# Sums of u and low parts of h in the second feed-forward: reordered between ScalarE and VectorE, first inner sums two products later

## The chip, the cores and the metric

The kernel runs on one NeuronCore of a Trainium2 chip. The metric is the device time of one execution in microseconds; the median of several runs stands for a kernel. TensorE (PE in the profile) multiplies matrices into PSUM banks, VectorE (DVE) and ScalarE (ACT) do the elementwise work, GpSimd (POOL) and SyncE (SP) mostly issue transfers. Each engine works through its own instructions in order and waits on semaphores for the others.

## The reference

One decoder block over 512 tokens of width 1024, all in float32: a SwiGLU feed-forward, a token mixer (pooling and dilated attention), and a second SwiGLU feed-forward, each on a modulated RMSNorm of the residual h, and a final RMSNorm. What the change touches is the feed-forward (inner width 2816):

```python
def swiglu(u, w_in, w_out):
    a, b = jnp.split(u @ w_in, 2, axis=-1)
    return (jax.nn.silu(a) * b) @ w_out

def reference(...):
    ...
    u = modulate(rmsnorm(h, g_norm_ffn2[l]), sh3, sc3)
    h = h + 0.5 * gt3 * swiglu(u, w_ffn2_in[l], w_ffn2_out[l])
    return rmsnorm(h, g_final)
```

## The kernel before

**Float32 products from high and low parts.** Every operand of TensorE is kept as a rounded part ("high", written by ScalarE as a copy to a narrower type) and the rest ("low", which VectorE gets by subtracting the high part). A product is three matmuls: high by high, high by low, low by high. So each weight tile costs one ScalarE copy (`whi`, line 312) and one VectorE subtraction (`wlo`, line 326), and so does each activation: u as `UH`/`UL`, the inner activation h as `HI`/`HK`. For weights of the second feed-forward that are not needed soon, ScalarE and a GpSimd transfer make the low part instead (line 308 and 310). All data is laid with features on the 128 partitions and the 512 tokens along the columns.

**A Strassen-like scheme with seven products.** Most inner tiles are not computed plainly. Two tiles at once (a "duo") are seen as a 2 by 2 block product, blocks of weights by blocks of u (two halves of the features by two halves of the tokens, 256 each). Instead of eight block products it needs seven, at the price of sums: four sums of weight blocks (line 251, VectorE, `X<-...`), four sums of blocks of u (line 699, once, since all duos share them), and the recombination of the results. The sums of u need high and low parts too: `SH`/`SL`, lines 705 and 706, and for the fourth one, which goes back into a part of `UH`/`UL`, lines 708 and 709. The second feed-forward does its output product in the same way ("quad", `out_quad`), from sums of four inner tiles ("inner sums", `h_sums`, lines 828 to 834), whose parts are `ut`, `G` and a half of `HI`/`HK`.

**The start of the second feed-forward** (`ffn2`). `head` computes four banks, the two halves a and b of inner tiles 0 and 1, plainly. Inner tiles 2 and 3 follow plainly (`ffn_tile`, 24 matmuls of 512 columns for each half), while VectorE forms the sums of u for the duos. For each of the tiles 0 to 3, `ffn_post` multiplies silu(a) by b on VectorE (`mult`, line 664), makes the high part on ScalarE (line 666) and the low part on VectorE (line 667). The list of steps that `u_steps` returns (first `whole`: u put together again from its parts for two blocks, line 715; then the four sums with their parts) is worked off between them: two steps after tile 0, three after tile 1, the rest while TensorE is in tile 2. The last step, the parts of the fourth sum, is called `last` and runs in the first duo after its product 0.

**The first duo** (inner tiles 4 and 5). Its seven products are numbered 0 to 6. They go to three PSUM banks A, B, C: A, B, A, C, A, B, A. After product 0 ScalarE copies A to C, after product 1 it copies B to SBUF (`p5`), after products 2 and 4 it copies A to SBUF (`u2`, `u3`: rows `u<-bank`), after 3 and 6 it takes the silu of C and A. The bank A goes on being accumulated, so product 2 can't begin before the copy of A to C is done, product 4 not before that of `u2`, product 6 not before that of `u3`.

**What sets the order.** The order is written by hand: each engine gets its instructions in the order in which the Python code issues them. `look` runs the weight splits three or four weight tiles ahead. `later(n, f)` puts work after the n-th product from now, and `step`, called after each product and ahead of that product's copies, runs what is due. `h_sums` puts its first sum at 2, and then one sum with the neighbouring high and low parts at each of 3 to 6. It is called once before the duo that comes ahead of each output quad: for quad 0 that is the first duo.

```python
        for n, what in enumerate(((lambda: add(h22, h21, h22, OP.add),),
                                  (lambda: high(0, h22), lambda: add(h21, h11, h21, OP.subtract), lambda: low(0, h22)),
                                  ...
            for f in what:
                self.later(2 + n, f)
```

Loads of weights are issued by SyncE into a few raw buffers. Two of them are the places of the blocks a12 and a22 of u; they can be used for weights once `last` is done.

The first feed-forward also calls `u_steps`; there one step is worked off after each of its first eight output tiles.

Of the kernel before, what the change touches and what calls it, by code (L numbers as in the profile page):

```python
# [11 lines left out]
AF = mybir.ActivationFunctionType  # L12
OP = mybir.AluOpType
# [130 lines left out]
class Kernel:  # L144
# [513 lines left out]

    def ffn_post(self, j, s, pb):
        nc = self.nc
        h = self.kept[j // 2 % 3][:, j % 2 * T:j % 2 * T + T] if self.kept else self.fw.tile([P, T], F32, name=("hf", "u3")[j % 2])
        nc.vector.tensor_tensor(h, s, pb, op=OP.mult)
        hh, hl = self.HH[j % NH], self.HL[j % NH]
        nc.scalar.activation(hh, h, AF.Copy)
        nc.vector.tensor_tensor(hl, h, hh, op=OP.subtract)

    def ffn_silu(self, j, pa):
        s = self.fw.tile([P, T], F32, name="sl" if j % 2 == 0 else "u2" if not self.kept else "p5")  # L670
# [22 lines left out]
    def u_steps(self, n):  # L693

        nc, v = self.nc, self.nc.vector
        (a11, a12), (a21, a22) = self.U4

        def add(o, x, y, op):
            return lambda: v.tensor_tensor(o, x, y, op=op)

        def split(i, u):
            def f():
                hi, lo = self.S[i]
                if i < 3:
                    nc.scalar.activation(hi, u, AF.Copy)
                    v.tensor_tensor(lo, u, hi, op=OP.subtract)
                    return
                nc.scalar.activation(hi, u.rearrange("p (k t) -> p k t", k=4), AF.Copy)
                v.tensor_tensor(lo, u.rearrange("p (k t) -> p k t", k=4), hi, op=OP.subtract)
            return f  # L710

        def whole(u, k):
            x = slice(k, k + 4)
            hi, lo = (y.rearrange("p (k t) -> p k t", k=KT)[:, x, :HT] for y in (self.UHv, self.ULv))
            return lambda: v.tensor_tensor(u.rearrange("p (k t) -> p k t", k=4), hi, lo, op=OP.add)

        last = split(3, a12)
        return ([whole(a11, 0), whole(a12, 4)] if n else []) + [add(a22, a21, a22, OP.add), split(0, a22), add(a21, a11, a21, OP.subtract), split(2, a21),
                add(a11, a22, a11, OP.subtract), split(1, a11), add(a12, a12, a11, OP.subtract)], last

    def step(self):

# [94 lines left out]
    def h_sums(self, k0):  # L817

        nc, v = self.nc, self.nc.vector
        half = lambda x, h: x.rearrange("p (j h t) -> p j h t", j=2, h=2)[:, :, h, :]  # L820
        a, b = (self.kept[k // 2 % 3] for k in (k0, k0 + 2))
        h11, h21, h12, h22 = half(a, 0), half(a, 1), half(b, 0), half(b, 1)
        x = slice(k0 % NH * T, (k0 % NH + 2) * T)
        r = lambda x: x.rearrange("p (j t) -> p j t", j=2)
        to = [(r(h), r(l)) for h, l in self.G] + [(half(self.HHall[:, x], 1), half(self.HLall[:, x], 1))]

        def add(o, x, y, op):
            v.tensor_tensor(o, x, y, op=op)

        def high(i, s):  # L830
            nc.scalar.activation(to[i][0], s, AF.Copy)

        def low(i, s):
            v.tensor_tensor(to[i][1], s, to[i][0], op=OP.subtract)

        for n, what in enumerate(((lambda: add(h22, h21, h22, OP.add),),
                                  (lambda: high(0, h22), lambda: add(h21, h11, h21, OP.subtract), lambda: low(0, h22)),
                                  (lambda: high(2, h21), lambda: add(h11, h22, h11, OP.subtract), lambda: low(2, h21)),
                                  (lambda: high(1, h11), lambda: add(h12, h12, h11, OP.subtract), lambda: low(1, h11)),
                                  (lambda: high(3, h12), lambda: low(3, h12)))):  # L840
            for f in what:
                self.later(2 + n, f)

    def out_quad(self, k0, gate):

# [56 lines left out]
    def ffn2(self):  # L902
        self.put, self.now = [], 0
        self.kept = [self.cond, self.cs, self.AR]
        bk = [self.nb() for _ in range(4)]
        self.head(2, bk, AF.Silu)
        self.G = [(self.tp.tile([P, T], F32R, name="ut"), self.fw.tile([P, T], F32R, name=f"G{i}")) for i in range(3)]
        self.todo, last = self.u_steps(2)
        do = lambda n: [self.todo.pop(0)() for _ in range(n)]
        for j in range(2):  # L910
            self.ffn_post(j, self.ffn_silu(j, bk[2 * j]), bk[2 * j + 1])
            do(2 + j)
        pa = self.ffn_tile()
        do(len(self.todo))
        self.ffn_post(2, self.ffn_silu(2, pa), self.ffn_tile())
        self.ffn_pair(3)
        self.ffn(2, 4, last)

    def open_ffn(self):
# [766 lines left out]
```

## Time and profile before

| | |
|---|---|
| median of 3 runs | 1012.51 us (1011.1 to 1012.77) |
| the profiled execution, its own time | 1010.66 us |
| its span in the profile | 1008.8 us |
| VectorE busy in the span | 788.6 us (78%) |
| ScalarE busy | 496.4 us (49%) |
| GpSimd busy | 47.3 us (5%) |
| chain of waits that ended last | TensorE 90%, VectorE 7%, ScalarE 1% |

TensorE is busy for nearly the whole span. Engine names in rows are PE, DVE, ACT, POOL and SP (SPq: SyncE's issues of transfers). In a timeline row stand the start in us, the duration, the engine, the line of the kernel, the operation, the tile that is written, the tiles that are read, and in brackets how long the engine was idle before and who ended that. A row of the list of waits has the total, the number of times and the longest. A row of a stretch has the length, the busy time of TensorE, its weight loads, VectorE, ScalarE and GpSimd with the number of instructions, then the granted clock of TensorE (1.00 is full), the busy share of the transfers, and GB/s.

### The profile page before, as it was taken

How to read it: one execution, taken by the hardware profiler on the slowest of the kernel's cores; microseconds unless marked ns; L12 is line 12 of the kernel's file. 1: busy time of each engine (PE TensorE's matmuls, PEld its weight loads, DVE VectorE, ACT ScalarE, POOL GpSimd, SP SyncE). 2: the span in 40 equal slices, each digit the busy share in tenths (PEclk: the TensorE clock that was granted, in tenths of full speed). 3: DMA queues.
4: the chain of work that ended last, by engine and by line, in shares of the span. 5: the costliest groups of instructions: out<-in, count | busy, mean ns of one | idle time of the engine just before them, and what ended most of it. 6: DMA issues, size and time to landing. Idle time of an engine off the chain costs nothing.

```text
span 1008.8 us, 16370 instructions
## 1 busy us (share of the span) xinstructions
PE 994.6 (99%) x6652; PEld 913.9 (91%) x6652; DVE 788.6 (78%) x1182; ACT 496.4 (49%) x754; POOL 47.3 (5%) x54
## 2 busy tenths in 40 slices
PE   8999999999999999999999999999899999999997
PEld 6888898989999999889988888898899999999996
DVE  7978879889787676879447777567998988989754
ACT  6443253625434552233414333463677768677652
POOL 0000000000000000007100000000011011011001
PEclk9999999999999999999999999999999999999998
DMA  9866456555533413122054774322467666756712
GB/s 341 275 224 228 140 195 189 175 164 185 168 99 117 145 46 99 58 84 84 32 185 161 272 261 134 92 78 63 146 147 178 177 147 155 201 130 164 178 32 84
DMA packets 46574, 152.24 MB, mean 151 GB/s; under 512 B 5281, under 2 KB 8609, under 8 KB 46498
## 3 DMA queue, kind: packets, MB, share of 16 engines
q1 hardware_dynamic: 42354, 137.95, 41.3%
q0 software_dynamic: 3456, 12.58, 7.5%
q8 instruction: 52, 0.85, 0.3%
q10 hardware_dynamic: 688, 0.66, 0.2%
q14 instruction: 24, 0.20, 0.1%
HBM read 148.40 MB, written 2.77 MB: 150 GB/s over the span
## 4 chain that ended last, share of the span: by engine, by line
PE 90%; DVE 7%; ACT 1%; issue 1%; DMA 0%; DVEq 0%; ACTq 0%
PE bank L357 14%; PE bank L358 14%; PE bank L359 14%; PE bank L739 10%; PE bank L741 9%; PE bank L740 9%; PE bank L867 3%; PE bank L866 3%; PE bank L865 3%; DVE wlo L326 1%; PE bank L1616 1%; PE bank L1620 1%; PE bank L1618 1%; PE bank L1212 1%; PE bank L1391 1%; PE bank L1392 1%
## 5 line engine op out<-in xcount | busy, mean ns | idle before, releaser
L326 DVE TENSOR_TENSOR wlo<-raw,whi 128x1024 fp32r<-128x1024 f32 (+7 forms) x157 | 156.7, 1011 | 56.0 <-ACT whi L312 55.8
L312 ACT ACTIVATE whi<-raw 128x1024 fp32r<-128x1024 f32 (+7 forms) x172 | 150.6, 894 | 31.2 <-DVE raw L251 27.6
L357 PE MATMUL bank<-UH,whi 128*128 128x512 f32 (+1 forms) x432 | 158.0, 366 | 0.0
L358 PE MATMUL bank<-UL,whi 128*128 128x512 f32 (+1 forms) x432 | 154.0, 357 | 0.1
L359 PE MATMUL bank<-UH,wlo 128*128 128x512 f32 (+1 forms) x432 | 153.9, 356 | 0.0
L741 PE MATMUL bank<-UH,wlo 128*128 128x256 f32 x512 | 141.6, 277 | 0.0
L739 PE MATMUL bank<-UH,whi 128*128 128x256 f32 x512 | 141.5, 276 | 0.0
L740 PE MATMUL bank<-UL,whi 128*128 128x256 f32 x512 | 141.5, 276 | 0.0
L326 DVE TENSOR_TENSOR wlo<-X,whi 128x1024 fp32r<-128x1024 f32 (+4 forms) x102 | 111.4, 1099 | 30.8 <-ACT whi L312 30.5
L312 ACT ACTIVATE whi<-X 128x1024 fp32r<-128x1024 f32 (+4 forms) x111 | 105.6, 966 | 40.6 <-DVE X L251 39.6
L739 PE MATMUL bank<-SH,whi 128*128 128x256 f32 x384 | 108.0, 281 | 3.0 <-ACT u L746 2.2
L740 PE MATMUL bank<-SL,whi 128*128 128x256 f32 x384 | 107.6, 280 | 0.0
L741 PE MATMUL bank<-SH,wlo 128*128 128x256 f32 x384 | 107.5, 280 | 0.0
L357 PE MATMUL bank<-HI,whi 128*128 128x512 f32 (+1 forms) x278 | 96.8, 348 | 0.0
L358 PE MATMUL bank<-HK,whi 128*128 128x512 f32 (+1 forms) x278 | 96.5, 347 | 0.0
L740 PEld LDWEIGHTS bank<-UL,whi 128*128 128x128 f32 x512 | 96.2, 188 | 0.2
L359 PE MATMUL bank<-HI,wlo 128*128 128x512 f32 (+1 forms) x278 | 96.4, 347 | 0.0
L741 PEld LDWEIGHTS bank<-UH,wlo 128*128 128x128 f32 x512 | 96.1, 188 | 0.2 <-DMA wlo<-wf2i 0.2
L739 PEld LDWEIGHTS bank<-UH,whi 128*128 128x128 f32 x512 | 96.1, 188 | 0.2
L359 PEld LDWEIGHTS bank<-UH,wlo 128*128 128x128 f32 x432 | 81.1, 188 | 12.1
L358 PEld LDWEIGHTS bank<-UL,whi 128*128 128x128 f32 x432 | 81.2, 188 | 11.7 <-issue 0.5
L357 PEld LDWEIGHTS bank<-UH,whi 128*128 128x128 f32 x432 | 81.2, 188 | 11.2 <-issue 0.5
(300 smaller groups left out, 2104.1 us busy)
## 6 DMA issues: line engine op xcount, KB each, us to landing
ada<-wada SPq DMA_DIRECT2D x47, 512.0 KB, 5.3
raw<-wmix SPq DMA_DIRECT2D x44, 512.0 KB, 4.1
raw<-wf1i SPq DMA_DIRECT2D x34, 512.0 KB, 4.5
raw<-wf2i SPq DMA_DIRECT2D x30, 512.0 KB, 3.7
wlo<-wf2i POOLq DMA_DIRECT2D x16, 512.0 KB, 6.3
X<-wf2i SPq DMA_DIRECT2D x14, 512.0 KB, 4.3
cs<-wada SPq DMA_DIRECT2D x12, 512.0 KB, 3.7
AR<-wada SPq DMA_DIRECT2D x12, 512.0 KB, 4.4
```

The source lines that it names most:

```text
L312: self.nc.scalar.activation(self.hi[:, y], r[:, x], AF.Copy)
L326: self.nc.vector.tensor_tensor(self.lo[:, y], r[:, x], self.hi[:, y], op=OP.subtract)
L357: M(ps, hi, uh, start=start, stop=False)
L358: M(ps, hi, ul, start=False, stop=False)
L359: M(ps, lo, uh, start=False, stop=stop)
L739: M(o, hi, uh, start=start and p == 0 and k == 0, stop=False, skip_group_check=True)
L740: M(o, hi, ul, start=False, stop=False, skip_group_check=True)
L741: M(o, lo, uh, start=False, stop=k == 3, skip_group_check=True)
L865: M(o, hi, uh, start=start and m % 2 == 0 and k == 0, stop=False, skip_group_check=True)
L866: M(o, hi, ul, start=False, stop=False, skip_group_check=True)
L867: M(o, lo, uh, start=False, stop=k == 1, skip_group_check=True)
L1212: M(o, pt[:, blk * P:blk * P + P], v, start=i == 0, stop=i == len(srcs) - 1)
```

## The change

The computation is the same. Three things move.

`ffn_post` takes a function `between`, which gets the low part of h as a thing to be done and decides when. For tiles 0 and 1 one step of the sums of u comes ahead of the low part; for tile 2 it comes after the first half of tile 3 has been issued, for tile 3 after product 0 of the first duo.

`u_steps` no longer issues the high and the low part of a sum one after the other: the high part is followed by the next sum, and the low part comes one step later. The number of steps stays, and so the first feed-forward gets the new order too.

`h_sums` starts after product 4 from its call instead of 2, for quad 0 alone.

```diff
-    def ffn_post(self, j, s, pb):
+    def ffn_post(self, j, s, pb, between=None):
...
         nc.scalar.activation(hh, h, AF.Copy)
-        nc.vector.tensor_tensor(hl, h, hh, op=OP.subtract)
+        low = lambda: nc.vector.tensor_tensor(hl, h, hh, op=OP.subtract)
+        if between is None:
+            return low()
+        between(low)
...
+        def high(i, u):
+            return lambda: nc.scalar.activation(self.S[i][0], four(i, u), AF.Copy)
+
+        def low(i, u):
+            return lambda: v.tensor_tensor(self.S[i][1], four(i, u), self.S[i][0], op=OP.subtract)
+
+        def both(*fs):
+            return lambda: [f() for f in fs]
...
-        return ([whole(a11, 0), whole(a12, 4)] if n else []) + [add(a22, a21, a22, OP.add), split(0, a22), add(a21, a11, a21, OP.subtract), split(2, a21),
-                add(a11, a22, a11, OP.subtract), split(1, a11), add(a12, a12, a11, OP.subtract)], last
+        return ([whole(a11, 0), whole(a12, 4)] if n else []) + [
+            add(a22, a21, a22, OP.add), both(high(0, a22), add(a21, a11, a21, OP.subtract)),
+            both(high(2, a21), low(0, a22)), add(a11, a22, a11, OP.subtract), both(high(1, a11), low(2, a21)),
+            add(a12, a12, a11, OP.subtract), low(1, a11)], both(high(3, a12), low(3, a12))
...
-                self.later(2 + n, f)
+                self.later((2 if k0 else 4) + n, f)
...
         for j in range(2):
-            self.ffn_post(j, self.ffn_silu(j, bk[2 * j]), bk[2 * j + 1])
-            do(2 + j)
+            self.ffn_post(j, self.ffn_silu(j, bk[2 * j]), bk[2 * j + 1], lambda low: (do(1), low(), do(1 + j)))
         pa = self.ffn_tile()
         do(len(self.todo))
-        self.ffn_post(2, self.ffn_silu(2, pa), self.ffn_tile())
-        self.ffn_pair(3)
+        due = []
+        self.ffn_post(2, self.ffn_silu(2, pa), self.ffn_tile(), due.append)
+        pa = self.ffn_tile()
+        due.pop()()
+        self.ffn_post(3, self.ffn_silu(3, pa), self.ffn_tile(), lambda low: self.later(1, low))
         self.ffn(2, 4, last)
```

How the instructions now stand shows at three places. The lines of the changed file are a few higher (699 is 702, 706 is 710, 746 is 750, 831 is 835).

VectorE at the start of the second feed-forward, from the first `whole` on, before (`cond` holds h of tiles 0 and 1, `X` the blocks of u, `HK`, `SL` and `wlo` are low parts):

```order
L715 TENSOR_TENSOR X<-UH,UL 128x1024 x2
L664 TENSOR_TENSOR cond<-p_5891,bank_100 128x512
L667 TENSOR_TENSOR HK<-cond,HI 128x512
L699 TENSOR_TENSOR X<-X 128x1024
L706 TENSOR_TENSOR SL_5609<-X,SH_5608 128x1024
L699 TENSOR_TENSOR X<-X 128x1024
L326 TENSOR_TENSOR wlo<-raw_67,whi 128x1024
L706 TENSOR_TENSOR SL_5614<-X,SH_5613 128x1024
```

And the same piece with the change:

```order
L718 TENSOR_TENSOR X<-UH,UL 128x1024
L667 TENSOR_TENSOR HK<-cond,HI 128x512
L718 TENSOR_TENSOR X<-UH,UL 128x1024
L664 TENSOR_TENSOR cond<-p_5891,bank_100 128x512
L702 TENSOR_TENSOR X<-X 128x1024
L667 TENSOR_TENSOR HK<-cond,HI 128x512
L702 TENSOR_TENSOR X<-X 128x1024
L710 TENSOR_TENSOR SL_5609<-X,SH_5608 128x1024
L326 TENSOR_TENSOR wlo<-raw_67,whi 128x1024
L702 TENSOR_TENSOR X<-X 128x1024
L710 TENSOR_TENSOR SL_5614<-X,SH_5613 128x1024
```

Between each multiplication or sum and its low part now stands one other operation.

ScalarE in the first duo, from the copy after product 1 (`p_6025`) to the silu after product 3 (`sl`), before; `ut` is the high part of an inner sum, `whi` that of a weight:

```order
L746 ACTIVATE p_6025<-bank_100 128x512
L312 ACTIVATE whi<-X 128x1024
L831 ACTIVATE ut<-cs 128x512
L746 ACTIVATE u_6026<-bank_99 128x2x256
L312 ACTIVATE whi<-X 128x1024
L831 ACTIVATE ut<-cond 128x512
L769 ACTIVATE sl<-bank_101 128x2x256
```

With the change, up to the copy after product 4 (the second `u_6025`):

```order
L750 ACTIVATE p_6024<-bank_100 128x512
L312 ACTIVATE whi<-X 128x1024
L750 ACTIVATE u_6025<-bank_99 128x2x256
L312 ACTIVATE whi<-X 128x1024
L773 ACTIVATE sl<-bank_101 128x2x256
L312 ACTIVATE whi<-X 128x1024
L835 ACTIVATE ut<-cs 128x512
L750 ACTIVATE u_6025<-bank_99 128x2x256
```

The high part of the first inner sum stood ahead of the copy after product 2 and now stands ahead of the copy after product 4.

ScalarE at the seam of the duo and the output quad, from the silu after product 6 to the quad's first copies from bank to bank (line 848), before:

```order
L769 ACTIVATE sl<-bank_99 128x2x256
L312 ACTIVATE whi<-X 128x896
L312 ACTIVATE whi<-X 128x128
L848 ACTIVATE bank_101<-bank_102 128x512
L848 ACTIVATE bank_100<-bank_97 128x512
```

With the change:

```order
L773 ACTIVATE sl<-bank_99 128x2x256
L312 ACTIVATE whi<-X 128x896
L312 ACTIVATE whi<-X 128x128
L835 ACTIVATE HI<-cs 128x2x256
L852 ACTIVATE bank_101<-bank_102 128x512
L852 ACTIVATE bank_100<-bank_97 128x512
```

The high part of the last inner sum has come in ahead of the two copies. TensorE, GpSimd and SyncE have the same instructions in the same order as before.

More of the change, by code (lines that the diff above doesn't have):

```diff
@@ L699, in add @@
             return lambda: v.tensor_tensor(o, x, y, op=op)
[L701 to L710, printed above, removed]
+        four = lambda i, u: u.rearrange("p (k t) -> p k t", k=4) if i == 3 else u
+        def high(i, u):
[4 more added lines that the diff above has]
+            return lambda: [f() for f in fs]
         def whole(u, k):
@@ L715, in whole @@
             return lambda: v.tensor_tensor(u.rearrange("p (k t) -> p k t", k=4), hi, lo, op=OP.add)
-        last = split(3, a12)
-        return ([whole(a11, 0), whole(a12, 4)] if n else []) + [add(a22, a21, a22, OP.add), split(0, a22), add(a21, a11, a21, OP.subtract), split(2, a21),
-                add(a11, a22, a11, OP.subtract), split(1, a11), add(a12, a12, a11, OP.subtract)], last
+        return ([whole(a11, 0), whole(a12, 4)] if n else []) + [
+            add(a22, a21, a22, OP.add), both(high(0, a22), add(a21, a11, a21, OP.subtract)),
+            both(high(2, a21), low(0, a22)), add(a11, a22, a11, OP.subtract), both(high(1, a11), low(2, a21)),
+            add(a12, a12, a11, OP.subtract), low(1, a11)], both(high(3, a12), low(3, a12))
     def step(self):
```

## The prediction

> **What bounds the kernel now.** I read the page first, then who waited for whom on TensorE, then the timeline of TensorE around the two waits found there.
>
> ```profile
> span 1008.8 us, 16370 instructions
> PE bank L1538 <- ACT cond L1536: 3.3, 1, 3.3
> PE bank L739 <- ACT u L746: 2.2, 1, 2.2
> PE bank L739 <- ACT bank L746: 0.8, 1, 0.8
> PE bank L1189 <- ACT prob L1177: 0.3, 1, 0.3
> PE bank L443 <- ACT ut L510: 0.3, 1, 0.3
> PE bank L1616 <- ACT UH L472: 0.3, 1, 0.3
> ```
>
> TensorE sets the end: all its listed waits make 7.2 us of 1008.8, so no reordering on other engines can be worth more than these and what hangs on them. The 3.3 us lie at the program's start. The 2.2 and 0.8 us lie in one place, the first duo of the second feed-forward, where the change works. Here are its products on TensorE (24 matmuls each, counted from 0): the first row opens product 0, 714.65 closes 1, 715.71 opens 2, 718.55 opens 3, 721.16 closes 3, 723.63 opens 4, 727.97 opens 5.
>
> ```profile
> 709.06 0.28 PE L739 MATMUL bank<-UH,whi 128*128 128x256 f32 x1
> 714.65 0.28 PE L741 MATMUL bank<-SH,wlo 128*128 128x256 f32 x1
> 715.71 0.38 PE L739 MATMUL bank<-SH,whi 128*128 128x256 f32 x1 [0.77 <-ACT bank L746]
> 718.55 0.28 PE L739 MATMUL bank<-UH,whi 128*128 128x256 f32 x1
> 721.16 0.28 PE L741 MATMUL bank<-UH,wlo 128*128 128x256 f32 x1
> 723.63 0.58 PE L739 MATMUL bank<-SH,whi 128*128 128x256 f32 x1 [2.19 <-ACT u L746]
> 727.97 0.28 PE L739 MATMUL bank<-UH,whi 128*128 128x256 f32 x1
> ```
>
> A matmul follows the last after about 0.11 us. So product 2 could have started at 714.77 and is 0.94 us late; product 4 could have started at 721.27 and is 2.36 us late. And product 4 itself takes 4.34 us (723.63 to 727.97), where product 3 took 2.72 (718.55 to 721.27): 1.62 us more. The slices of 1 us tell why; the column to read is the granted clock, before "DMA share".
>
> ```profile
> 723.00:724.00 1.00, 0.37 (x1) 0.37 (x2) 1.00 (x2) 1.00 (x3) 0.00 (x0) 0.72 0.95 389
> 724.00:725.00 1.00, 1.00 (x6) 1.00 (x6) 1.00 (x3) 1.00 (x3) 0.00 (x0) 0.50 1.02 418
> 726.00:727.00 1.00, 1.00 (x7) 1.00 (x7) 1.00 (x2) 0.99 (x1) 0.00 (x0) 0.57 0.62 250
> 727.00:728.00 1.00, 1.00 (x11) 1.00 (x11) 1.00 (x3) 0.33 (x1) 0.00 (x0) 1.00 0.07 29
> ```
>
> Behind the long pause the clock is 0.50 for some 3 us. The place costs 0.94 + 2.36 + 1.62 = 4.92 us.
>
> What is late is ScalarE, and behind it VectorE:
>
> ```profile
> 713.59 0.63 ACT L666 ACTIVATE HI<-cs 128x512 fp32r<-128x512 f32 x1 [1.89 <-DVE cs L664]
> 715.07 0.58 ACT L746 ACTIVATE bank<-bank 128x512 f32<-128x512 f32 x1
> 720.72 1.06 ACT L312 ACTIVATE whi<-X 128x1024 fp32r<-128x1024 f32 x1 [1.63 <-DVE X L251]
> 722.46 0.63 ACT L831 ACTIVATE ut<-cs 128x512 fp32r<-128x512 f32 x1 [0.68 <-DVE cs L828]
> 723.00 0.58 ACT L746 ACTIVATE u<-bank 128x512 f32<-128x512 f32 x1
> ```
>
> The copy that product 2 needs (715.07) stands behind the high part of h of tile 3 (713.59), which waits for VectorE's multiplication. The copy that product 4 needs (723.00) stands behind a weight split (720.72) and the high part of the first inner sum (722.46), both waiting for VectorE. VectorE in its turn had waited for ScalarE six times before (first two rows: total, times, longest, from 684 to 740 us; then the operations that the walk below starts from and compares with):
>
> ```profile
> DVE HK L667 <- ACT HI L666: 2.8, 4, 0.7
> DVE SL L706 <- ACT SH L705: 2.3, 2, 1.2
> 687.09 0.69 DVE L664 TENSOR_TENSOR cond<-sl,bank 128x512 f32<-128x512 f32 x1 [1.26 <-ACT sl L671]
> 688.47 0.69 DVE L667 TENSOR_TENSOR HK<-cond,HI 128x512 fp32r<-128x512 f32 x1 [0.70 <-ACT HI L666]
> 689.08 2.36 DVE L715 TENSOR_TENSOR X<-UH,UL 128x1024 f32<-128x1024 f32 x2
> 695.75 1.23 DVE L706 TENSOR_TENSOR SL<-X,SH 128x1024 fp32r<-128x1024 f32 x1 [1.19 <-ACT SH L705]
> 705.12 1.23 DVE L251 TENSOR_TENSOR X<-raw,raw 128x1024 f32<-128x1024 f32 x1
> 712.87 0.68 DVE L664 TENSOR_TENSOR cs<-p,bank 128x512 f32<-128x512 f32 x1
> 719.47 1.22 DVE L251 TENSOR_TENSOR X<-raw,X 128x1024 f32<-128x1024 f32 x1
> 721.74 0.68 DVE L828 TENSOR_TENSOR cs<-cond,cs 128x512 f32<-128x512 f32 x1
> ```
>
> These 5.1 us are the pattern "ScalarE copies the high part, VectorE at once subtracts it".
>
> **The change part by part.** No instruction is added or removed; TensorE, GpSimd and SyncE keep their order. I walk VectorE's new order from 687.09 with its own spacings: 1.14 us from start to start for 1024 columns (2.36 for two, less 1.22), 0.61 for 512 (688.47 to 689.08), and 1.06 and 0.63 us for ScalarE's copies.
>
> *Low parts one operation later, pairs 0 and 1.* Multiplication 687.09, first u half 687.70, low part of h 688.84 (its high part ended at 688.44, so no wait), second half 689.45, multiplication 690.59, sum a22 691.20, low part 692.34 (high part done at about 691.9), sum a21 692.95, low part of a22 694.09. The waits of 0.70, 0.70 and 1.19 us are gone.
>
> *What stands in their place.* On ScalarE the high part of a21 now comes ahead of a weight copy. It starts when a21 is done (694.2) and the weight copy runs from 695.2 to 696.2. VectorE, free at 695.2, loses 1.0 us there. Then a11 at 697.4, low parts and a12 without a wait, and the weight subtraction that was at 705.12 starts at 702.0: 3.1 us earlier.
>
> *Pairs 2 and 3.* The two waits of 0.70 become two of about 0.6 (now the weight's low part waits for its copy, which stands behind h's high part). Multiplication 3, at 712.87 before, comes at 709.6. Its tile is ready: the matmul before 709.06 was its last, and ran out at 709.2. So the high part of h is done at 710.9, the weight copy at 711.9, and the copy of product 0 runs from its end (about 712.1) to 712.7. Product 2 may start at 714.77: wait 1 goes, 2.1 us to spare.
>
> *Inner sums two products later.* From 709.6 follow seven operations and a 0.6 us wait, and the weight subtraction of 719.47 starts at 716.0. ScalarE's weight copy ends at 718.3 and the copy for product 4 follows it at once, without the sum ahead: 718.3 to 718.9. Product 4 is due at 714.77 + 2.84 + 2.72 = 720.3 (the two durations of products 2 and 3): wait 2 goes, 1.4 us to spare. Without this part it would be nearer: sum and high part stood 2.3 us (720.72 to 723.00) before the copy.
>
> *Where the sums go.* The first now stands five operations behind that weight subtraction (two before): 716.0 + 5 x 1.14 = 721.7 (721.74 before, but TensorE is now ahead). Its high part ends at 723.0 and the copy for product 6 runs 723.2 to 723.8; product 6 is due at 725.7. The last sum starts at 729.9, behind ten operations. ScalarE does a weight split, then its high part, then the two copies of the output quad, until about 733.0. The quad's product 2, which needs them, is due nine products after 709.06, with 2.72 to 2.84 us each at 733.6 to 734.6. This 0.6 to 1.6 us is the thinnest margin.
>
> *Loads.* Two operations later in the walk VectorE needs two loads that SyncE issues once the low part of a12 frees the buffers:
>
> ```profile
> 718.42 0.80 SPq L235 DMA_DIRECT2D X<-wf2o  x2
> 724.68 1.22 DVE L251 TENSOR_TENSOR X<-X 128x1024 f32<-128x1024 f32 x1
> ```
>
> They took at most 6.3 us from issue (VectorE came to the sum without a wait). The low part now ends at 714.9, so the loads land by 721.2 at the latest, and the sum is wanted at 719.5. At best it costs nothing, at worst everything behind is 1.7 us late, and the quad waits for at most 1.1 us. I take nothing, since the row has only the upper bound and margins cover the middle; the 1.1 us goes into the range.
>
> *First feed-forward.* The same sums are reordered there. The list of TensorE's waits has none of its output tiles, so VectorE's three waits there, like the following, are idle time that costs nothing: zero.
>
> ```profile
> 94.39 1.23 DVE L706 TENSOR_TENSOR SL<-X,SH 128x1024 fp32r<-128x1024 f32 x1 [0.46 <-ACT SH L705]
> ```
>
> *The clock.* I count the 1.62 us as gained, since the clock falls in the very slice in which TensorE starts again after 2.36 us of pause, and nothing like it follows the 0.94 us pause (product 2 took 2.84). The Trainium skill, "TensorE: Matmul & The Clock Gate" (Part 1), has the clock halved after about one idle window of 3.4 us and restored after as long a stretch of work. The trace agrees on the return (0.50 until about 726.8, 3.2 us after 723.63), not on the length of the pause. By that rule a pause of 2.36 us need not be the cause, and the sum would be 3.30 instead of 4.92.
>
> **The sum.** The profiled execution took 1010.66 us (its span and 1.86 around it), below the median of the runs, 1012.51. 1010.66 - 4.92 = 1005.74; the same off the median gives 1007.6, which I forecast.
>
> **The rivals.**
> - *The clock is not the pause's* (0.10). Both waits go, the slow stretch stays or falls elsewhere: 1012.51 - 3.30 = 1009.2. Against it: the slices around 723.
> - *A smaller wait in the output quad* (0.12). VectorE gains 3.1 to 3.5 us, TensorE 4.92, so TensorE runs 1.4 to 1.8 us closer to VectorE. It waits 1.1 us by the loads' bound, and up to 1.8 if the quad has no margin at all: 1008.7 to 1009.4. For it: the thin margin and the loads' bound. Against it: the walk.
> - *No change* (0.08). The lateness is handed on until TensorE has waited for all of it somewhere behind the quad: 1012.5. VectorE gets only the 3 us, so every margin behind would have to be near nothing; but in the output quad, whose copies stand in the same queue, TensorE has no wait in the list.
> - *Slower* (0.08). One mechanism: in ScalarE's queue the high part of the last inner sum now stands directly ahead of the quad's bank copies, so VectorE's lateness holds up TensorE there. A pause s costs s, and 1.62 more once it is near 2.4 us. It decides against the change from s + 1.62 = 4.92, so s = 3.3 us, which with the margin's middle of 1.1 is 4.4 us of slip; at s = 5.5 the time is 1012.51 - 4.92 + 7.12 = 1014.7. For it: VectorE is busy 1.00 in all the slices shown around 724, so it can't make up. Against it: the loads can slip by 1.7 us only.
>
> **How the numbers follow.** The forecast has the remaining 0.62, with a range of its own of 1006.2 to 1008.5 (runs spread from 1011.1 to 1012.77 around their median). With the two partial cases 0.84 lies between 1005.8 and 1010.2: the lower end is 1007.6 less the spread and some, the upper 1009.4 and some 0.8 us for the runs' spread. A measurement here tells 0.2% (2 us) from no change. Forecast, clock and quad cases are all beyond it: faster 0.84, same 0.08, slower 0.08.
>
> **What would show it.** Right: no wait of L739's successor for a ScalarE copy in the list, the seven products of the duo within about 19.5 us, granted clock 1.00 in every slice there; VectorE's waits for h's high parts and for SH gone, but one of about 1.0 us at a weight's low part behind the sums of u; the copy for product 4 done before product 3 ends. The quad case shows as a wait of the quad's product 2 for a bank copy; the clock case as a slice below 0.9 without a pause ahead. Wrong would be any pause over 2 us between the duo and the end of the first quad.

## The result and the profile after

| | before | changed |
|---|---|---|
| median (6 runs each) | 1012.22 us (1011.1 to 1013.77) | 1007.6 us (1006.82 to 1010.1) |
| ratio, 95% interval | | 0.9953 (0.994 to 0.9966) |
| the profiled execution, its own time | 1010.66 us | 1007.38 us |
| its span | 1008.8 us | 1005.6 us |

The kernel is faster by 0.47% (0.34 to 0.6%, or 3.4 to 6.1 us). Timed again beside 24 runs of before it gave 1008.62 against 1012.51, 0.996 (0.9946 to 0.9975).

First the span, the busy times and the chain of the profile's page after the change:

```profile
span 1005.6 us, 16371 instructions
PE 993.2 (99%) x6652; PEld 912.9 (91%) x6652; DVE 788.0 (78%) x1182; ACT 496.1 (49%) x754; POOL 47.3 (5%) x54
PE 92%; DVE 4%; DMA 2%; ACT 1%; issue 0%; DVEq 0%; ACTq 0%
```

VectorE's and ScalarE's busy times are those of before within 0.6 us: nothing became cheaper, only waits moved. VectorE's share of the chain went from 7% to 4%, TensorE's from 90% to 92%, and a transfer now has 2%. The list of TensorE's waits names it (us in total, times, longest):

```profile
PE bank L1544 <- ACT cond L1542: 3.3, 1, 3.3
PE bank L871 <- DMA wlo<-wf2o: 1.0, 2, 0.8
```

Both waits of the first duo (2.2 and 0.8 us, at line 739, now 743) are gone. New is one of 0.8 us at line 871, a product of the output quad, for a weight's low part that a GpSimd transfer brings. On TensorE's timeline after (start, duration, and in brackets the idle time before) the first row opens the duo, the next two open its products 2 and 4, and the last two lie in the quad's product 5:

```profile
709.39 0.28 PE L743 MATMUL bank<-UH,whi 128*128 128x256 f32 x1
715.09 0.28 PE L743 MATMUL bank<-SH,whi 128*128 128x256 f32 x1
720.55 0.28 PE L743 MATMUL bank<-SH,whi 128*128 128x256 f32 x1
742.43 0.28 PE L870 MATMUL bank<-HK,whi 128*128 128x256 f32 x1
743.54 0.39 PE L871 MATMUL bank<-HI,wlo 128*128 128x256 f32 x1 [0.84 <-DMA wlo<-wf2o]
```

Product 4 opens 11.16 us after the duo, where it took 14.57 before (709.06 to 723.63). The 3 us ahead of it and behind it are busy throughout and at full clock (the column before the DMA share):

```profile
718.00:721.00 3.00, 3.00 (x28) 3.00 (x28) 2.81 (x3) 2.34 (x4) 0.00 (x0) 1.00 0.98 378
721.00:724.00 3.00, 3.00 (x29) 3.00 (x28) 3.00 (x4) 2.31 (x4) 0.00 (x0) 1.00 0.97 362
```

VectorE's timeline shows which waits are left around the sums: one behind the copies of `SH`, at a weight's low part, of 0.94 us; multiplication 3 starts at 709.80, 3.07 us earlier than before:

```profile
687.41 0.69 DVE L664 TENSOR_TENSOR cond<-sl,bank 128x512 f32<-128x512 f32 x1 [1.26 <-ACT sl L674]
689.15 0.68 DVE L667 TENSOR_TENSOR HK<-cond,HI 128x512 fp32r<-128x512 f32 x1
696.51 1.23 DVE L326 TENSOR_TENSOR wlo<-raw,whi 128x1024 fp32r<-128x1024 f32 x1 [0.94 <-ACT whi L312]
702.31 1.22 DVE L251 TENSOR_TENSOR X<-raw,raw 128x1024 f32<-128x1024 f32 x1
709.80 0.68 DVE L664 TENSOR_TENSOR cs<-p,bank 128x512 f32<-128x512 f32 x1
716.40 1.22 DVE L251 TENSOR_TENSOR X<-raw,X 128x1024 f32<-128x1024 f32 x1
720.17 1.23 DVE L251 TENSOR_TENSOR X<-X 128x1024 f32<-128x1024 f32 x1 [0.19 <-DMA X<-wf2o]
722.45 0.68 DVE L832 TENSOR_TENSOR cs<-cond,cs 128x512 f32<-128x512 f32 x1
730.61 0.68 DVE L832 TENSOR_TENSOR cs<-cs,cond 128x512 f32<-128x512 f32 x1
```

ScalarE's timeline shows the copies for product 4 (718.62) and product 6 (723.71), and at the end the high part of the last inner sum, the quad's bank copies and the ScalarE half of the low part in question:

```profile
717.65 1.06 ACT L312 ACTIVATE whi<-X 128x1024 fp32r<-128x1024 f32 x1 [1.16 <-DVE X L251]
718.62 0.58 ACT L750 ACTIVATE u<-bank 128x512 f32<-128x512 f32 x1
723.17 0.63 ACT L835 ACTIVATE ut<-cs 128x512 fp32r<-128x512 f32 x1 [0.67 <-DVE cs L832]
723.71 0.58 ACT L750 ACTIVATE u<-bank 128x512 f32<-128x512 f32 x1
731.84 0.62 ACT L835 ACTIVATE HI<-cs 128x512 fp32r<-128x512 f32 x1
732.36 1.06 ACT L852 ACTIVATE bank<-bank 128x512 f32<-128x512 f32 x2
733.35 1.06 ACT L308 ACTIVATE wlo<-raw 128x1024 fp32r<-128x1024 f32 x1
```

So the copy for product 4 is done at 719.20, 1.35 us before product 4 opens.

**Where the time went.** Between the same matmuls of TensorE's timeline, the stretch from the duo's opening to the end of the quad's product 0 (709.06 to 736.12 before) took 27.06 us and now takes 22.04: 5.02 gained. From there to the sixth matmul of the next duo (736.12 to 753.01 before) it took 16.89 and now takes 18.02: 1.13 given back. That is 3.9 us net. The spans differ by 3.2, since this execution began its work 0.3 us later and lost another 0.4 between 800 and 860 us.

Why the quad gives something back shows at that transfer. Before, these are GpSimd's issue (start, duration), the time from the issue to the landing of the data (last number, from the list of transfers), and the matmul on TensorE that needs the data:

```profile
738.69 0.86 POOL L310 DMA_DIRECT2D wlo<-wf2o  x1 [4.58 <-ACT wlo L308]
wlo<-wf2o POOLq DMA_DIRECT2D x1, 512.0 KB, 7.6
747.23 0.28 PE L867 MATMUL bank<-HI,wlo 128*128 128x256 f32 x1
```

After, the matmul is the one at 743.54 shown above:

```profile
734.71 0.86 POOL L310 DMA_DIRECT2D wlo<-wf2o  x1 [5.73 <-ACT wlo L308]
wlo<-wf2o POOLq DMA_DIRECT2D x1, 512.0 KB, 8.8
```

Before, the data landed at about 746.3, 0.9 us ahead of the matmul that needs them. Now the issue comes 3.98 us earlier, but without a wait that matmul would have come 4.69 us earlier (at 742.54, 0.11 us after the one at 742.43). This takes 0.7 us of the 0.9. The transfer itself took 1.2 us longer, so the data landed at 743.5 and the matmul is 1.0 us late. With the 7.6 us of before they would have been there in time.

### The profile page after: what moved, and what is told of

Its sections match the earlier page's. It is cut to its first block, busy times and chain, and to the rows that moved or that the text cites. A ratio compares the mean times of both kernels' runs of the same rounds, so it can differ in the third digit from the quotient of the medians.

```text
span 1005.6 us, 16371 instructions
## 1 busy us (share of the span) xinstructions
PE 993.2 (99%) x6652; PEld 912.9 (91%) x6652; DVE 788.0 (78%) x1182; ACT 496.1 (49%) x754; POOL 47.3 (5%) x54
## 4 chain that ended last, share of the span: by engine, by line
PE 92%; DVE 4%; DMA 2%; ACT 1%; issue 0%; DVEq 0%; ACTq 0%
PE bank L357 15%; PE bank L358 15%; PE bank L359 15%; PE bank L743 10%; PE bank L745 10%; PE bank L744 10%; PE bank L871 2%; PE bank L869 2%; PE bank L870 2%; DMA wlo<-wf2o 2%; PE bank L1622 1%; PE bank L1624 1%; PE bank L1626 1%; PE bank L1218 1%; PE bank L1397 1%; PE bank L1398 1%
```

## The experiments

The table has for each kernel the two stretches above from its own profile (the duo with the quad's product 0; the rest of the quad, with the first five matmuls behind it), and the time against before from runs on the same chip.

| kernel | duo, us | rest of quad, us | median, us | ratio (95%) |
|---|---|---|---|---|
| before | 27.06 | 16.89 | | |
| changed | 22.04 | 18.02 | 1007.6 | 0.9953 (0.994 to 0.9966) |
| changed, again | 22.05 | 17.94 | 1008.62 | 0.996 (0.9946 to 0.9975) |
| reorder only | 22.19 | 18.28 | 1008.51 | 0.9954 (0.9939 to 0.9969) |
| later sums only | 25.12 | 18.90 | 1012.6 | 1.0002 (0.9991 to 1.0014) |
| u sums in the old order | 22.05 | 18.53 | 1008.93 | 0.9958 (0.9943 to 0.9973) |
| low parts of h in the old order | 22.80 | 19.00 | 1010.21 | 0.9976 (0.9965 to 0.9986) |
| first feed-forward in the old order | 22.04 | 17.06 | 1008.41 | 0.9958 (0.9943 to 0.9973) |
| last inner sum one later | 22.05 | 18.27 | 1008.64 | 0.9959 (0.9944 to 0.9974) |
| inner sums spread | 22.05 | 17.21 | 1007.74 | 0.9955 (0.9939 to 0.9971) |
| low part by VectorE | 22.05 | 16.89 | 1009.03 | 0.9966 (0.9952 to 0.9979) |

### Which part of the change does it

**The reorder without the later inner sums**, against the changed kernel:

```diff
-                self.later((2 if k0 else 4) + n, f)
+                self.later(2 + n, f)
```

> The change without its third part: low parts and sums of u in the new order, inner sums at 2 as before. My theory (VectorE's six waits for ScalarE made both pauses): the multiplication of tile 3 still comes near 709.8, wait 1 (0.94 us) is gone, wait 2 is at most 0.4 us instead of 2.36, since VectorE's first inner sum is done some 3.3 us earlier and TensorE only 0.94 us; no slice under clock 0.9; in the quad a wait of 0.8 to 1.3 us for a low part that comes by GpSimd's transfer. About 4 us faster than before (1008.2 off 1012.2). Rival (the place of the inner sums made wait 2): wait 2 stays near 2 us with the slow clock behind it, 1 to 1.5 us faster than before (1011).

Its ScalarE timeline at the copy for product 4 (start, duration, idle time before):

```profile
717.91 1.07 ACT L312 ACTIVATE whi<-X 128x1024 fp32r<-128x1024 f32 x1 [1.16 <-DVE X L251]
719.64 0.63 ACT L835 ACTIVATE ut<-cs 128x512 fp32r<-128x512 f32 x1 [0.67 <-DVE cs L832]
720.18 0.58 ACT L750 ACTIVATE u<-bank 128x512 f32<-128x512 f32 x1
```

The sum's high part is back ahead of the copy, which ends at 720.76. Product 4 opens at 720.82: just in time, no wait in the duo, and the ratio is that of the change. With both halves of the reorder the later sums aren't needed; they buy slack (0.06 us here, 1.35 with them). This was the expected outcome.

**The later inner sums without the reorder**, against before:

```diff
-                self.later(2 + n, f)
+                self.later((2 if k0 else 4) + n, f)
```

> The kernel before with the third part alone: inner sums of the first quad at 4, everything else as before. My theory: wait 1 stays (0.9 to 1.1 us), wait 2 shrinks by the sum and its high part, to about 1.2 us; whether the clock falls then is open, if it does not, this shows that the fall belongs to the longer pause; in the quad waits for GpSimd's transfers of up to 1.5 us in all. About 1 to 2 us faster than before (1010.2 to 1011.2). Rival (the place of the inner sums made wait 2): wait 2 gone, some 4 us faster (1008.2).

The list of TensorE's waits, without its 3.3 us at the start:

```profile
PE bank L739 <- ACT u L746: 1.3, 2, 0.7
PE bank L867 <- DMA wlo<-wf2o: 1.0, 1, 1.0
PE bank L739 <- ACT bank L746: 0.7, 1, 0.7
PE bank L865 <- ACT bank L848: 0.2, 1, 0.2
```

And one row of VectorE's timeline:

```profile
725.75 1.23 DVE L251 TENSOR_TENSOR X<-X 128x1024 f32<-128x1024 f32 x1 [1.45 <-DMA X<-wf2o]
```

No gain. The long pause ahead of product 4 is cut (0.85 us late), the clock stays at 1.00, and the duo is 1.94 us shorter; but product 6 is now 0.79 late, and the quad, with a bank copy and the transfer, 2.01 longer. VectorE still has its waits of 2.8 us for h's high parts and 2.3 for `SH`, so its lateness remains. A new wait comes with it: VectorE, with the inner sums out of its way, gets to a weight sum before the load for it has landed, and waits 1.45 us (the row at 725.75; before, it came there without a wait). The copy for product 6 stands behind the work that this delays. TensorE pays in five small waits in place of two. An expected gain of 1 to 2 us did not come.

**The sums of u in the old order**, the rest changed (`u_steps`):

```diff
-            add(a22, a21, a22, OP.add), both(high(0, a22), add(a21, a11, a21, OP.subtract)),
-            both(high(2, a21), low(0, a22)), ...
+            add(a22, a21, a22, OP.add), both(high(0, a22), low(0, a22)), add(a21, a11, a21, OP.subtract),
+            both(high(2, a21), low(2, a21)), ...
```

> The change with the sums of u back in their old order (high and low part of a sum at once); low parts of h late and inner sums at 4 as in the change. My theory: VectorE's two waits for SH (2.3 us) come back and its 0.94 us wait for the weight copy goes, so it is about 1.3 us later than in the change, which the spare 2.1 and 1.35 us cover: both pauses stay away; the transfer wait in the quad grows from 0.84 to 1.3 us or a second small one joins it. 0 to 1 us slower than the change. Rival (the sums of u carry half of the gain): a wait of over 1 us at product 2 or 4, 2 us or more slower than the change.

**The low parts of h in the old order**, the rest changed (`ffn_post` subtracts at once for all four tiles):

```diff
-            self.ffn_post(..., lambda low: (do(1), low(), do(1 + j)))
+            self.ffn_post(..., lambda low: (low(), do(2 + j)))
...
-        self.ffn_post(2, self.ffn_silu(2, pa), self.ffn_tile(), due.append)
...
-        self.ffn_post(3, self.ffn_silu(3, pa), self.ffn_tile(), lambda low: self.later(1, low))
+        self.ffn_post(2, self.ffn_silu(2, pa), self.ffn_tile())
+        self.ffn_pair(3)
```

> The change with the low parts of h at once as before; sums of u in the new order and inner sums at 4 as in the change. My theory: four waits of 0.70 us come back and two of 0.5 go, VectorE is about 1.8 us later than in the change, so product 4 waits 0.4 to 1.0 us, without a slow clock, and the transfer wait in the quad is 1.3 us or more: 1 to 2.5 us slower than the change. Rival (the low parts of h don't matter): no wait in the duo, same as the change.

VectorE's start of multiplication 3 in the kernel with the old u sums, and then in the one with the old low parts of h:

```profile
711.59 0.68 DVE L664 TENSOR_TENSOR cs<-p,bank 128x512 f32<-128x512 f32 x1
```

```profile
712.69 0.68 DVE L664 TENSOR_TENSOR cs<-p,bank 128x512 f32<-128x512 f32 x1
```

Both kernels did what was expected of them. The duos open at 710.22 and 710.33 in these, so the multiplication comes 1.37 and 2.36 us into the duo, against 3.81 before and 0.41 with the change. At 1.37 the duo loses nothing (22.05). At 2.36 product 4 waits, as the list of TensorE's waits in the kernel with the old low parts shows:

```profile
PE bank L871 <- DMA wlo<-wf2o: 1.3, 1, 1.3
PE bank L743 <- ACT u L750: 0.5, 1, 0.5
PE bank L745 <- DMA wlo<-wf2i: 0.7, 2, 0.4
```

The h low parts are thus needed for the full gain, the order of u's sums is not: without it the ratio can't be told from the change's. With h in the old order about half the gain stays: product 4 is 0.65 us late, not 2.36, and the clock stays at 1.00. That half comes from the order of u's sums, since the later inner sums alone gave 1.0002. So the two halves overlap: each moves VectorE forward, and beside the h half the u half has nothing left to gain. Both kernels have the later inner sums; no kernel has one half without them.

### The first feed-forward

Against the changed kernel, `u_steps` in the old order in the first feed-forward alone:

```diff
+        if not n:
+            both2 = lambda i, u: both(high(i, u), low(i, u))
+            return [add(a22, a21, a22, OP.add), both2(0, a22), ...], both(high(3, a12), low(3, a12))
```

> The change with the first feed-forward's sums of u in their old order. My theory: VectorE waits there three times 0.47 us again, TensorE does not wait for any of it: same as the change within 0.5 us, and TensorE's list of waits has nothing new before 240 us. Rival: the first feed-forward gave part of the gain, 0.5 us or more slower than the change.

VectorE's list of waits between 40 and 140 us has the three waits for `SH` back:

```profile
DVE SL L710 <- ACT SH L707: 1.4, 3, 0.5
```

TensorE has none that belongs to them, and the ratio doesn't move: that part is worth zero.

### What the quad gives back

**The change itself once more**, with no edit:

> The change itself, once more, beside the next ones on one chip. My theory: as before, 4 to 5 us faster than the kernel before (1008), no wait in the duo, one wait of 0.8 to 1.2 us in the first quad's product 5 for the low part that comes by GpSimd's transfer.

Its wait in the quad is there too (0.73 us late). The issue and, on TensorE, the matmul that needs the data:

```profile
735.83 0.86 POOL L310 DMA_DIRECT2D wlo<-wf2o  x1 [5.72 <-ACT wlo L308]
```

```profile
744.29 0.38 PE L871 MATMUL bank<-HI,wlo 128*128 128x256 f32 x1 [0.56 <-DMA wlo<-wf2o]
```

**The last inner sum one product later**, so that its high part no longer stands ahead of the quad's bank copies and of the transfer's ScalarE half:

```diff
-                self.later((2 if k0 else 4) + n, f)
+                self.later((2 if k0 else 4) + n + (n == 4 and not k0), f)
```

> The change with the high and low part of the last inner sum one product later, behind the first quad's bank copies on ScalarE. My theory (the low part that GpSimd's transfer completes is late because ScalarE starts it late, behind that high part, 0.52 us): ScalarE's start for the second transfer comes 0.5 us earlier and the wait of 0.84 us falls to 0.3 to 0.5; 0.4 to 0.6 us faster than the change in the profile, too little for the times. Rival (the transfer is late because the transfers compete, not because it starts late): the wait stays at 0.8 us or more.

The wait was expected to fall to 0.3 to 0.5 us; it didn't. The issue moved by only 0.15 us (25.17 us into the duo, 25.32 in the change), since the second bank copy now waited for VectorE (0.17 us), and the wait grew, to 1.27 us:

```profile
744.87 0.39 PE L871 MATMUL bank<-HI,wlo 128*128 128x256 f32 x1 [1.10 <-DMA wlo<-wf2o]
```

That is 9.25 us after the issue at 735.62. In the three runs with the change's order in the second feed-forward (the change, the change again, the first feed-forward undone) the data came 8.83, 8.46 and at most 7.89 us after an issue that stood 25.3 to 25.4 us into the duo; in the last TensorE didn't wait at all. So the transfer's own time, with one order, decides whether the quad gives back 0 or 1.1 us.

**The inner sums spread** over products 4, 5, 7, 8, 9:

```diff
-                self.later((2 if k0 else 4) + n, f)
+                self.later(2 + n if k0 else [4, 5, 7, 8, 9][n], f)
```

> The change with the first quad's inner sums at 4, 5, 7, 8 and 9 instead of 4 to 8, so that VectorE and ScalarE come to the weights of that quad earlier. My theory: both starts of the transfers come earlier by 0.5 to 1 us, the quad's wait is gone or under 0.2 us, no new wait for a sum's part: 0.8 to 1.1 us faster than the change (1006.8 off 1007.6), 5 us or more faster than before. Rival (the transfers compete): the wait stays and nothing is won. Second rival: the sums' parts are now late for the quad's products 2 and 4, a wait of 0.3 us or more for G or ut.

The issue came 24.25 us into the duo and the first quad had no wait for it, but later work had some (list of TensorE's waits). The time can't be told from the change's, where 0.8 to 1.1 us less was expected:

```profile
PE bank L745 <- DMA wlo<-wf2i: 0.7, 1, 0.7
PE bank L871 <- DMA wlo<-wf2o: 0.2, 1, 0.2
```

**That low part by VectorE** instead of the transfer:

```diff
                 self.outer.update({len(self.order) + 3: n + 3, len(self.order) + 5: n + 2})
+                if len(self.outer) == 2:
+                    del self.outer[len(self.order) + 5]
```

> The change with the second low part of the first quad made by VectorE's subtraction instead of ScalarE's negated copy and GpSimd's adding transfer. My theory (what is given back in the quad is this one transfer, which lands 7.8 to 9.2 us after its issue, sometimes too late): from the quad's second product to the next duo TensorE takes 16.9 to 17.1 us, as in the kernel before, instead of 17.9 to 18.0 in the change; a smaller wait of up to 0.5 us for the next transfer (a weight of the next duo) can follow, since VectorE has one operation more. Up to 1 us faster than the change. Rival (VectorE is the limit there): 17.9 us or more again, with a wait for VectorE or ScalarE in the place of the transfer.

The rest of the quad takes 16.89 us, as before the change: this shows that the give-back is the wait for this transfer. This was expected, but the timed ratio is no better than the change's. A gain of 1 us lies inside the intervals, so no version here is shown to beat the change.

### The clock

Three kernels add idle ScalarE copies (four, five and six) to the changed kernel, ahead of the copy for product 4 of the first duo, to make TensorE pause there. Each ran once (1009.46, 1010.1 and 1014.05 us, against 1012.45 for before); the third's duo opens 3.4 us later than the change's (712.77 against 709.39), so the duos are compared and not the times. Here with four:

```diff
+                for _ in range(4 if self.kept and j == 4 else 0):
+                    copy(self.tr[:, :4 * P], self.tr[:, :4 * P])
                 copy(u2, r(A))
```

> The change with four idle ScalarE copies of 512 columns (on a scratch tile, nothing else reads it) right ahead of the copy that product 4 waits for. They take 2.1 to 2.6 us, of which 1.35 are spare: a pause of 0.8 to 1.3 us in the duo. My theory (a pause over about 2 us halves the clock, a shorter one doesn't): clock 1.00 behind it, duo longer by the pause alone. Rival (any pause at this place lowers the clock): a slice near 0.5 behind it.

> The same with five copies: a pause of 1.3 to 1.9 us, between what is seen to leave the clock alone (0.94) and what halved it (2.36). Open which; this shows on which side of the bound it is. The rule of 3.4 us: clock 1.00.

> The same with six copies: a pause of 1.9 to 2.6 us. My theory (the 1.62 us of the sum hang on the pause): clock near 0.5 for some 3 us behind it, as in the kernel before, and the duo is longer by the pause and 1.3 to 1.7 us. By the rule of 3.4 us, and by the rival that the fall in the kernel before had another cause: clock 1.00, the duo longer by the pause alone.

Product 4 was 1.22, 1.87 and 2.55 us late, and the duo longer than the change's 22.04 by 1.34, 2.00 and 4.17. The first two cost their length and 0.12 to 0.13 us (behind the pause product 4 takes 2.84 us, not 2.72); the third costs 1.62 more than its length, of which 1.50 are the clock's if the same 0.12 belongs to the restart. One-microsecond slices of the kernel with five copies, and then of the one with six (granted clock before the DMA share):

```profile
723.00:724.00 1.00, 0.73 (x6) 0.74 (x7) 0.00 (x0) 1.00 (x2) 0.00 (x0) 1.00 1.00 401
724.00:725.00 1.00, 1.00 (x11) 1.00 (x11) 0.81 (x1) 1.00 (x3) 0.00 (x0) 1.00 0.45 180
```

```profile
726.00:727.00 1.00, 0.53 (x2) 0.53 (x3) 0.00 (x0) 1.00 (x2) 0.00 (x0) 0.64 0.94 385
727.00:728.00 1.00, 1.00 (x7) 1.00 (x6) 0.60 (x1) 1.00 (x3) 0.00 (x0) 0.50 0.24 98
728.00:729.00 1.00, 1.00 (x7) 1.00 (x7) 1.00 (x2) 0.80 (x1) 0.00 (x0) 0.50 0.02 8
729.00:730.00 1.00, 1.00 (x7) 1.00 (x7) 1.00 (x2) 0.63 (x1) 0.00 (x0) 0.65 0.44 102
730.00:731.00 1.00, 1.00 (x11) 1.00 (x10) 1.00 (x2) 0.00 (x0) 0.00 (x0) 1.00 0.91 283
```

So the long pause brings the slow clock, at this place in the program. A length at which it falls is not shown: each length was profiled once. Finer slices show the fall inside the pause, not at its end: at 723.44 in before, where product 4 opens at 723.63, and at 726.29 with six copies, where it opens at 726.48. In both the clock stays at 0.50 for 3.41 us. It also was at 0.50 for 3.41 us from 13.45 us on in the repeat of the change, where the list of TensorE's waits has nothing over 0.2 us between 3.3 us and there. In before, the clock's next change behind 726.85, at the program's end (1003.33), comes 276.48 us later, which is 81 times 3.413. This suggests that the clock is set anew every 3.41 us from how busy TensorE was, so that the place of a pause could count beside its length; no kernel here moves a pause of the same length.

## Why the prediction was right, and where it was not

The duo's sum was right: 4.92 us forecast, 5.02 measured. The 0.10 us between them are product 2's: its 2.84 us behind the pause were taken as its normal length, and without the pause it takes 2.74.

- *Low parts one operation later.* The waits for h's high parts and `SH` went, as said. The prediction had priced both halves together. The kernels that undo one half each show that, with the later inner sums, the h half is enough for the whole gain, and the u half alone for about half of it (0.9976).
- *What stands in their place.* A VectorE wait of 1.0 us that ends at 696.2 was forecast; it came as 0.94 and ended at 696.51, and the weight subtraction forecast for 702.0 came at 702.31. In this execution the whole stage is 0.33 us later (709.39 against 709.06), so up to here the walk was right to 0.1 us. Further on it drifts: the first and the last inner sum, forecast for 721.7 and 729.9, came at 722.45 and 730.61, 0.4 us later than the shift explains.
- *Inner sums two products later.* The copy for product 4 was forecast for 718.3 with 1.4 us to spare, and started at 718.62 with 1.35. But the text let this part look like a condition of wait 2's end: "Without this part it would be nearer". By the experiments it is neither needed (reorder alone: same ratio) nor worth anything alone (1.0002, 0.9991 to 1.0014). Cutting up the long pause alone gains nothing, because VectorE's lateness, and a load that is now wanted too early, are then paid a little later.
- *Where the sums go.* The quad's bank copies were to end by about 733.0; they ended at 733.42 (732.36 and 1.06), and TensorE had no wait for them. The thin margin held.
- *Loads.* Taken as zero between 0 and 1.7 us; VectorE waited 0.19. The risk was real: in the kernel with only the later sums the same wait was 1.45.
- *First feed-forward.* Zero, shown.
- *The clock.* The 1.62 us were counted as the pause's. The kernel with six copies makes that pause again (2.55 us) and loses 1.62 again; pauses of 1.87 and less lose 0.13 at most beside their length. So the pause is the cause here. The Trainium skill, "TensorE: Matmul & The Clock Gate" (Part 1), puts the fall after an idle window of about 3.4 us; here 2.36 and 2.55 us were enough, so the measurement decides, and the rival with 1009.2 falls. What the page says of the return agrees (0.50 for 3.41 us, 3.2 of them with TensorE at work).
- *The step that failed: no loss in the output quad.* The quad does give back 1.1 us in this profile, the size that the rival with the smaller wait had (1.1 to 1.8), but neither at the bank copies nor by the late loads that it named. The walk followed VectorE's and ScalarE's instructions up to the bank copies and stopped there. The ScalarE half of the quad's low part stands right behind them, and the transfer behind it gained 3.98 us, where its user on TensorE gained 4.69. It had only 0.9 us to spare before, which a list of waits can't show: the working should have compared its landing (738.69 and 7.6) with its user (747.23). By that 0.2 us would have been left; the rest of the loss is that the transfer took 8.8 us this time, which the traces of before could not tell.

The forecast of 1007.6 is the measured median, but 1 us of this agreement is the spread of the runs: duo and quad net 3.9 us in the profile where 4.92 were forecast, and the second measurement has 1008.62. The range holds both. That the two meet to the tenth is luck. Not settled is why the transfer took 7.6 us in before, 7.9 in one kernel with the change's order and 8.8 in the change. Two loads of raw weights are issued within 2 us behind it, but before the change too, and no kernel was run without them.

## What to carry to other kernels

When two engines hand work back and forth, take the waiting out of the engine that is late (let one other operation stand between a producer on one engine and its consumer on the other), and don't just move the work that stands in the way: that alone gave 1.0002 here. When a stretch becomes faster, follow every producer of the next stretch up to its user, transfers included, and compare how much each of them gained with how much its user gained and what it had to spare: TensorE waits next where the spare is used up. And when a pause on TensorE can't be removed, it is worth making it shorter than the 2.4 us that cost 1.62 us more here: pauses up to 1.87 us kept the clock at 1.00, in one profile each. The time saved stays saved only if the work behind it is ready too, as the kernel with only the later sums shows.

## What the hardware showed beyond that

- The clock fell to 0.50 for 3.41 us within pauses of 2.36 and 2.55 us, at a price of 1.62 us each beside the pause, and not at pauses of 0.65 to 1.87 us. It fell 0.19 us before TensorE went on.
- One transfer with accumulation (512 KB, issued by GpSimd) landed 7.6 us after its issue in before and 7.9 to 9.2 us after it in the other kernels that have it; with the same order in the second feed-forward it was 7.9, 8.4 and 8.8.
- An early matmul of the program (17.87 us from the start in before) ran between 17.9 and 21.9 us in the profiles of these kernels, though nothing ahead of it was changed. TensorE was slower there: twelve small matmuls (`H` by `ones`) took 1.50 us in before (from 14.17) and 2.72 in the kernel with the old first feed-forward (from 17.47), one of the latest. The spread is as much as the gain itself, so stages are better compared by the starts of the same matmuls than by spans.
